# Operands of the split matmuls moved to multiples of 512 bytes, and the merge stage of a hybrid layer reordered

## The chip, the cores and the metric

The kernel runs on one core of one Trainium2 chip. The metric is device time in microseconds (us) of one launch, as the median of several runs. A separate execution was recorded by the hardware profiler; all rows below come from that one. Engines are named as in the profile: PE is the matmul engine TensorE, PEld its weight loads, DVE is VectorE, ACT is ScalarE, POOL is GpSimd, and SP (SyncE) issues most of the DMAs.

## What is computed

One layer over 1024 tokens of width 1024, in fp32: a swiglu feed-forward block (FFN1, inner width 2816), a mixer with two branches (an RWKV-7 recurrence and dilated causal attention) whose outputs are gated and merged, a second swiglu block (FFN2), and a small gated embedding term at the end. The part around the reordering is this:

```python
x = x + 0.5 * swiglu(rms_norm(x, ffn1_norm), ffn1_w_gate, ffn1_w_up, ffn1_w_down)
h = rms_norm(x, mix_norm)
z_rwkv, z_attn, z_gate = jnp.split(h @ w_in, [RWKV_COLS, RWKV_COLS + ATTN_COLS], axis=-1)
y_rwkv = rwkv7_time_mix(z_rwkv, ...)
y_attn = dilated_attention_mix(z_attn, cos, sin, q_gain, k_gain)
g_rwkv, g_attn = jnp.split(jax.nn.sigmoid(z_gate), 2, axis=-1)
merged = g_rwkv * (y_rwkv @ w_br_rwkv) + g_attn * (y_attn @ w_br_attn)
x = x + merged @ w_out
x = x + 0.5 * swiglu(rms_norm(x, ffn2_norm), ffn2_w_gate, ffn2_w_up, ffn2_w_down)
```

## The kernel before, in words

**Split matmuls.** A large fp32 matmul is done as three in the type fp32r. An operand is stored as two tiles side by side: `split` lets ACT copy the value into the high part, and DVE or POOL subtract that from the value to get the low part (lines 236 and 237). `mm3` (lines 252 to 254) then multiplies high by high, high by low and low by high into one bank of PSUM. Weights pass through `wchunk`: a DMA on SP into the staging tile `wst`, which has two buffers, then `split` into `wsp` (or `wo`, for the output projection) with POOL doing the low part. FFN weights are loaded into `wr` and split into `wsp` too, some of them after sums of two. Activations lie in tiles `h`, `a`, `f` and `ya`. In the profile `g<-h,wsp` names the PSUM tile written, then the moving operand, then the stationary one.

**Where tiles start.** Tiles are laid one after another in each partition of SBUF, pool by pool. Several pools hold small tiles whose row is not a multiple of 512 bytes long (`nss` and `nrsy` of 16 bytes, `omu`, `carry`, `n2` and others), and they move what lies behind them. In the built program all split operands start 32, 160 or 480 bytes past a multiple of 512: `wsp` and `a` at 32; `h`, `f`, `ya` at 480; `wo`, `pT` and the embedding's operands at 160. Some stationary `h` operands are read with a stride of four columns and then start at 480, 484, 488 or 492.

**Order.** A planner, `weave`, advances several streams of Python generators and lets each emit its next piece; a piece yields its cost on PE and off PE in us, written by hand, and streams "F" are dense matmul work, the others small work. The result is then a fixed list of instructions for each engine.

**The merge** has three streams. `branch_r` multiplies the RWKV output with `w_br_rwkv`: eight blocks `b` of 128 columns in two halves of 512 tokens, each with 12 matmuls, whose result DVE multiplies by the gate in line 1696, after a load of that half of the gate into a tile `gst`. `attn_combine` (lines 1650 to 1664) writes the combine weights `f` to DRAM, loads them back as a broadcast `fb`, and DVE and POOL sum three attention outputs `ob` into `ya`, which is split. `merge_a` multiplies `ya` with `w_br_attn`, again eight blocks in two halves: six matmuls, DVE's gating (line 1721), POOL's addition of the other branch (line 1724), then the split into `h`, at once. The planner is told 1.3 us on PE and 2.6 off PE a block. In the second half each second block also loads and splits a piece of `w_out` into `wo`:

```python
G.tensor_tensor(out=s, in0=th, in1=rp, op=ALU.add)
mT[b][hf] = self.half(h2, b, hf)
self.split(mT[b][hf], s)
if hf and b % 2:
    out["W"].append(self.wcol(a["w_out"], 0, b // 2, op, "wo", 4))
yield 1.3, 2.6
```

`out_proj` comes after the merge: for two halves `n` of the columns and eight tiles `i` of 128 tokens, 24 matmuls `dn<-wo,h` each into one of three `dn` banks.

## Time and profile before

| | |
|---|---|
| median of 3 runs | 2764.57 us (2763.26 to 2764.85) |
| profiled execution, its own time | 2758.78 us |
| its span, first to last instruction | 2757.0 us |
| mean granted TensorE clock, of full | 0.960 |
| PE busy | 2557.2 us, 93% of the span, 14541 matmuls |
| PE weight loads busy | 2038.9 us, 74% |
| DVE busy | 1578.3 us, 57% |
| ACT busy | 972.9 us, 35% |
| POOL busy | 1147.6 us, 42% |
| moved by DMA | 289.19 MB |

Busy means that an instruction of the engine was under way. Matmuls follow each other in a pipeline, so the profile's duration of one is longer than the time from its start to the next one's, and PE counts as busy without being at its peak. The stages in time: FFN1's up-projection from 130 to 505 us, its down-projection to 720, the mixer from 800 to 1720, the merge from 1770 to 1850, the output projection to 1942, FFN2's up-projection from 2015 to 2405, its down-projection to 2630, the embedding term to the end.

### The profile page before, as it was taken

What the parts mean: (1) busy time and instruction counts of PE and PEld (TensorE: products, weight loads), DVE (VectorE), ACT (ScalarE), POOL (GpSimd) and SP (SyncE); (2) the same over time, 40 slices, a digit from 0 to 9 for tenths busy, and PEclk for the clock granted to TensorE, in tenths of its full rate; (3) what the DMA queues carried; (4) which work ended last, traced back from release to release, by engine and by line L of the source; (5) the groups of instructions that cost most, each with busy time, mean ns of one, the idle gap of its engine ahead of it and who ended that gap; (6) DMA issues with size and microseconds to landing.
All of it is one profiled execution on the core that took longest, in us unless ns stands there. A gap on an engine that the chain in (4) does not pass through costs nothing. (4 is left out here: it accounts for less than half of the span.)

```text
span 2757.0 us, 37053 instructions
## 1 busy us (share of the span) xinstructions
PE 2557.2 (93%) x14541; PEld 2038.9 (74%) x14541; DVE 1578.3 (57%) x2511; ACT 972.9 (35%) x1700; POOL 1147.6 (42%) x643
## 2 busy tenths in 40 slices
PE   7799999999999999889989998979799999989899
PEld 5688888777777666667876998658578888767777
DVE  4865455888715555554356335461875455578852
ACT  6333333333434323332324343421533333333541
POOL 2665555454424333332232213160565555554540
PEclk9999999999999998999989999899899999999999
DMA  5332222736333222222231101662132223363532
GB/s 185 92 91 70 84 77 92 279 119 214 129 109 89 56 65 56 65 59 54 76 111 47 59 32 55 193 222 73 44 103 77 85 77 92 129 227 117 176 122 92
DMA packets 273651, 289.19 MB, mean 105 GB/s; under 512 B 46410, under 2 KB 202668, under 8 KB 273220
## 3 DMA queue, kind: packets, MB, share of 16 engines
q1 hardware_dynamic: 266084, 274.59, 31.3%
q10 hardware_dynamic: 7392, 12.23, 1.3%
q8 instruction: 114, 1.87, 0.3%
q14 instruction: 61, 0.50, 0.1%
HBM read 222.64 MB, written 64.14 MB: 104 GB/s over the span
## 5 line engine op out<-in xcount | busy, mean ns | idle before, releaser
L237 POOL TENSOR_TENSOR wsp<-wr,wsp 128x1024 fp32r<-128x1024 f32 (+1 forms) x158 | 348.0, 2210 | 400.7 <-ACT wsp L236 361.7
L237 POOL TENSOR_TENSOR wsp<-wst,wsp 128x1024 fp32r<-128x1024 f32 x71 | 173.5, 2447 | 423.9 <-ACT wsp L236 406.9
L237 POOL TENSOR_TENSOR wsp<-ws,wsp 128x1024 fp32r<-128x1024 f32 x88 | 223.3, 2538 | 214.6 <-ACT wsp L236 210.6
L252 PE MATMUL g<-h,wsp 128*128 128x512 f32 x496 | 222.7, 449 | 8.5 <-DVE h L1696 6.7
L252 PE MATMUL g<-wsp,h 128*128 128x256 f32 (+1 forms) x664 | 216.4, 326 | 12.8 <-ACT raw L1416 11.4
L254 PE MATMUL g<-wsp,h 128*128 128x256 f32 (+1 forms) x664 | 206.4, 311 | 0.0
L253 PE MATMUL g<-wsp,h 128*128 128x256 f32 (+1 forms) x664 | 206.3, 311 | 0.0
L253 PE MATMUL g<-h,wsp 128*128 128x512 f32 x496 | 203.1, 409 | 0.0
L254 PE MATMUL g<-h,wsp 128*128 128x512 f32 x496 | 203.1, 409 | 0.0
L394 DVE TENSOR_TENSOR ws<-wr 128x512 f32<-128x512 f32 x56 | 86.5, 1553 | 197.2 <-POOL x L237 195.8
L236 ACT ACTIVATE wsp<-ws 128x1024 fp32r<-128x1024 f32 (+1 forms) x110 | 106.3, 967 | 197.7 <-PE dn L254 81.6
L236 ACT ACTIVATE wsp<-wr 128x1024 fp32r<-128x1024 f32 (+1 forms) x158 | 133.5, 851 | 96.6 <-DVE wr L738 37.9
L252 PE MATMUL dn<-wsp,h 128*128 128x512 f32 x360 | 145.0, 407 | 13.1 <-DVE x L779 5.5
L252 PEld LDWEIGHTS g<-wsp,h 128*128 128x128 f32 x664 | 137.5, 207 | 25.2 <-ACT raw L1416 12.0
L253 PE MATMUL dn<-wsp,h 128*128 128x512 f32 x360 | 144.7, 402 | 4.7 <-POOL wsp L237 4.5
L254 PE MATMUL dn<-wsp,h 128*128 128x512 f32 x360 | 143.7, 401 | 0.0
L253 PEld LDWEIGHTS g<-wsp,h 128*128 128x128 f32 x664 | 137.9, 208 | 3.9 <-issue 0.2
L254 PEld LDWEIGHTS g<-wsp,h 128*128 128x128 f32 x664 | 137.2, 207 | 4.1 <-issue 0.2
L252 PEld LDWEIGHTS g<-h,wsp 128*128 128x128 f32 x496 | 96.3, 194 | 42.4 <-issue 9.0
L254 PE MATMUL tr<-h,wsp 128*128 128x512 f32 x320 | 126.4, 395 | 0.0
L254 PE MATMUL dn<-h,wsp 128*128 128x512 f32 x320 | 126.3, 395 | 0.0
L252 PE MATMUL tr<-h,wsp 128*128 128x512 f32 x320 | 126.3, 395 | 0.0
(465 smaller groups left out, 6639.2 us busy)
## 6 DMA issues: line engine op xcount, KB each, us to landing
wr<-ffn_w_down SPq DMA_DIRECT2D x44, 1024.0 KB
wst<-w_in SPq DMA_DIRECT2D x60, 512.0 KB
wr<-ffn_w_gate SPq DMA_DIRECT2D x44, 512.0 KB
wr<-ffn_w_up SPq DMA_DIRECT2D x44, 512.0 KB
actD<-act SPq DMA_DIRECT2D x44, 512.0 KB
a<-actD SPq DMA_DIRECT2D x12, 1024.0 KB
gate<-gst SPq DMA_DIRECT2D x26, 256.0 KB
wst<-ffn_w_down SPq DMA_DIRECT2D x10, 512.0 KB
```

The source lines that it names most:

```text
L236: nc.scalar.activation(dst[:, 0], src, AF.Copy)
L237: (lo_eng or nc.vector).tensor_tensor(out=dst[:, 1], in0=src, in1=dst[:, 0].bitcast(F32), op=ALU.subtract)
L252: mm(ps, lhsT=l[0], rhs=r[0], start=first, stop=False)
L253: mm(ps, lhsT=l[0], rhs=r[1], start=False, stop=False)
L254: mm(ps, lhsT=l[1], rhs=r[0], start=False, stop=last)
L394: self.nc.vector.tensor_tensor(out=out, in0=R[:, i], in1=R[:, j], op=op)
```

## The change

Small tiles leave the pools that hold split operands: they go to the constants' pool `cp` or to the pool `hp` that lives through the kernel, or are made 64 columns wide of which a few are used. After that every split operand starts at a multiple of 512 bytes (the stationary ones read with a stride of four at 0, 4, 8 or 12 past one). `pi`, the token positions, is loaded at the start in place of in the mixer.

In `branch_r` the gate comes in whole blocks of 1024 tokens, one block ahead, through the staging tile `wst`. In `merge_a` the splits of a block are emitted after the next block's addition; in the first half DVE adds and not POOL; the pieces of `w_out` are loaded in the first half; and the planner is told 0.4 us off PE. A new stream, `out_early`, computes three output-projection tiles once the first half of the merge is done, and `out_proj` takes these as they are.

```diff
+def later(cond, make):
+    yield cond
+    yield from make()
...
-        y = self.t(pool, shape, tag + "y")
-        u = self.t(pool, shape, tag + "u")
+        if tag == "grs":
+            y, u = self.t(self.cp, shape, "grsy"), self.t(self.hp, shape, "grsu")
+        elif tag == "ars":
+            y, u = (self.t(self.hp, shape, tag + n) for n in "yu")
+        elif tag == "nrs":
+            y, u = (self.t(pool, [P, 64], tag + n)[:, :shape[1]] for n in "yu")
+        else:
+            y = self.t(pool, shape, tag + "y")
+            u = self.t(pool, shape, tag + "u")
...
-            self.ss = self.t(sp, [P, 4], "nss", bufs=2)
+            self.ss = self.t(sp, [P, 64], "nss", bufs=2)[:, :4]
...
-        omu = self.t(sp, [P, 14], "omu")
+        omu = self.t(self.cp, [P, 14], "omu")
...
-        carry = {}
+        carry = self.t(self.cp, [P, 14], "carry")
...
-        nb = self.t(sp, [64, 16], "nb")
+        nb = self.t(self.hp, [64, 16], "nb")
...
-        pi = self.t(sp, [P, NT], "pi", dt=I32)
+        pi = self.t(self.hp, [P, NT], "pi", dt=I32)
...
+        def tanh(b):
+            t = self.t(self.wp, [P, T], "wst", bufs=2)
+            nc.sync.dma_start(t, gateD[b])
+            return t
+
+        th = tanh(0)
...
+            nxt = tanh(b + 1) if b < KB - 1 else None
...
-                th = self.t(mx, [P, HALF], "gst2", bufs=2)
-                nc.sync.dma_start(th, gateD[b, :, hf * HALF:(hf + 1) * HALF])
+                hsl = slice(hf * HALF, (hf + 1) * HALF)
...
-                nc.vector.scalar_tensor_tensor(out=rp[b // 2][hf][:, b % 2], in0=th, scalar=1.0, in1=ps, op0=ALU.add,
+                nc.vector.scalar_tensor_tensor(out=rp[b // 2][hf][:, b % 2], in0=th[:, hsl], scalar=1.0, in1=ps, op0=ALU.add,
                                                op1=ALU.mult)
...
+            th = nxt
...
+        last = None
+
+        def finish():
+
+            b, hf, s = last
+            mT[b][hf] = self.half(h2, b, hf)
+            self.split(mT[b][hf], s)
+            if b == KB - 1:
+                out["mT", hf] = True
...
-                G.tensor_tensor(out=s, in0=th, in1=rp, op=ALU.add)
-                mT[b][hf] = self.half(h2, b, hf)
-                self.split(mT[b][hf], s)
-                if hf and b % 2:
+                (G if hf else V).tensor_tensor(out=s, in0=th, in1=rp, op=ALU.add)
+                if last:
+                    finish()
+                last = b, hf, s
+                if hf == 0 and b % 2:
                     out["W"].append(self.wcol(a["w_out"], 0, b // 2, op, "wo", 4))
-                yield 1.3, 2.6
+                yield 1.3, 0.4
+        finish()
         out["merged"] = True
+
+    def out_early(self, mT, pp, out):
+
+        yield lambda: ("mT", 0) in out
+        W = out["W"]
+        for i in range(3):
+            ps = self.t(pp, [P, HALF], "dn", bufs=3)
+            for kb in range(KB):
+                w = W[kb // 2][:, :, kb % 2]
+                self.mm3(ps, self.hs(mT, kb, i * P, P), (w[:, 0], w[:, 1]), kb == 0, kb == KB - 1)
+                yield 0.65, 0
+            out["early"][i] = ps
...
-    def out_proj(self, mT, x, W, sp, pp, ready):
+    def out_proj(self, mT, x, W, early, sp, pp, ready):
...
-                ps = self.t(pp, [P, HALF], "dn", bufs=3)
-                for kb in range(KB):
-                    w = W[n][kb // 2][:, :, kb % 2]
-                    self.mm3(ps, self.hs(mT, kb, i * P, P), (w[:, 0], w[:, 1]), kb == 0, kb == KB - 1)
+                if n == 0 and i in early:
+                    ps = early[i]
+                else:
+                    ps = self.t(pp, [P, HALF], "dn", bufs=3)
+                    for kb in range(KB):
+                        w = W[n][kb // 2][:, :, kb % 2]
+                        self.mm3(ps, self.hs(mT, kb, i * P, P), (w[:, 0], w[:, 1]), kb == 0, kb == KB - 1)
...
-                   ["F", self.merge_a(ya, h2, D_["gate"], wr, out, op)], br], lambda: "merged" in out)
+                   ["F", self.merge_a(ya, h2, D_["gate"], wr, out, op)], br,
+                   ["F", later(lambda: out["mT"] is not None and ("mT", 0) in out, lambda: self.out_early(out["mT"], pp, out))]],
+                  lambda: "merged" in out and len(out["early"]) == 3)
...
+    k.hp = hp
```

(`cp` and `hp` get more tiles in the same way: `hw0`, `ka2`, `rki`, `n2`, `bon`, `PC`, `gst` of the group norm, `gvar`, `pf`, `ass`, `nm`. The PSUM pool of the `dn` banks is opened ahead of the merge.)

Three places show how instructions move. A name ends in the buffer's number; what stands in brackets is the counters that a row waits for. First PE near the end of the merge. In the kernel before, the last `ya` blocks (`g<-ya,wsp`) and the output projection's first tile (`dn<-wo,h`) stand like this:

```order
L252 MATMUL g_15208<-ya_2268_14796,wsp_14827 128x512
L253 MATMUL g_15208<-ya_2268_14796,wsp_14827 128x512
L254 MATMUL g_15208<-ya_2268_14796,wsp_14827 128x512
L253 MATMUL dn_15279<-wo_15162,h_2307_15045 128x512 [waits Pool_49]
L254 MATMUL dn_15279<-wo_15162,h_2307_15045 128x512
L252 MATMUL dn_15279<-wo_15162,h_2309_15057 128x512
L253 MATMUL dn_15279<-wo_15162,h_2309_15057 128x512
L254 MATMUL dn_15279<-wo_15162,h_2309_15057 128x512
L252 MATMUL dn_15279<-wo_15191,h_2311_15069 128x512 [waits Activation_49]
L252 MATMUL g_15225<-ya_2267_14795,wsp_14827 128x512 [waits DVE_49]
L253 MATMUL g_15225<-ya_2267_14795,wsp_14827 128x512
L254 MATMUL g_15225<-ya_2267_14795,wsp_14827 128x512
```

In the changed kernel, PE at the same place, with two tiles in work (`dn_15139` and `dn_15253`):

```order
L265 MATMUL dn_15139<-wo_15122,h_2311_15136 128x512 [waits Activation_49]
L266 MATMUL dn_15139<-wo_15122,h_2311_15136 128x512
L267 MATMUL dn_15139<-wo_15122,h_2311_15136 128x512
L265 MATMUL dn_15253<-wo_15062,h_2293_15057 128x512
L265 MATMUL g_15220<-ya_2252_14781,wsp_14813 128x512 [waits DVE_49]
L266 MATMUL g_15220<-ya_2252_14781,wsp_14813 128x512
L267 MATMUL g_15220<-ya_2252_14781,wsp_14813 128x512
L265 MATMUL g_15220<-ya_2253_14782,wsp_14813 128x512
L266 MATMUL g_15220<-ya_2253_14782,wsp_14813 128x512
L267 MATMUL g_15220<-ya_2253_14782,wsp_14813 128x512
L265 MATMUL g_15235<-ya_2252_14781,wsp_14813 128x512 [waits DVE_49]
```

Seven `dn` matmuls stood ahead of the last `ya` block before; now 31 do, all 24 of the first tile and seven of the second.

Second, SP's queue from the attention outputs `ob` to the first broadcasts `fb`. Before:

```order
L1630 DMA ob_14799<-o_3562 128x3x512 [waits DMAHW4_49]
L1630 DMA ob_14801<-o_3562 128x3x512 [waits DMAHW5_49,DMAHW0_49]
L1690 DMA gst_2281_14850<-gate_3560 128x512 [waits DMAHW1_49,DVE_49]
L1690 DMA gst_2283_14866<-gate_3560 128x512 [waits DMAHW2_49,DVE_49]
L1650 DMA f_3564<-ce_14806 32x3x128 [waits DVE_49]
L1715 DMA wr_15034<-gate_3560 128x4x512 [waits PE_49]
L1690 DMA gst_2285_14882<-gate_3560 128x512 [waits DMAHW1_49,DVE_49]
L1659 DMA fb_14894<-f_3564 64x3x512 [waits DMAHW6_49,DMAHW3_49]
L1659 DMA fb_14894<-f_3564 64x3x512 [waits DMAHW7_49]
```

Changed, where `wst<-gate` is a whole gate block of `branch_r`:

```order
L257 DMA wst_14806<-w_br_attn 128x2x512 [waits DVE_49]
L1661 DMA f_3564<-ce_14792 32x3x128 [waits DMAHW5_49,DVE_49]
L257 DMA wst_14811<-w_br_attn 128x2x512
L1744 DMA wr_15008<-gate_3560 128x4x512 [waits PE_49]
L1698 DMA wst_14820<-gate_3560 128x1024 [waits DMAHW4_49,Pool_49]
L1670 DMA fb_14876<-f_3564 64x3x512 [waits DMAHW5_49,DMAHW1_49]
L1670 DMA fb_14876<-f_3564 64x3x512 [waits DMAHW2_49]
L1698 DMA wst_14850<-gate_3560 128x1024 [waits DMAHW3_49,DMAHW0_49,DVE_49]
L1670 DMA fb_14912<-f_3564 64x3x512 x2
```

Both loads of `w_br_attn` and a gate block that waits for a counter of POOL now stand ahead of the first `fb`; the two `gst` loads between are gone, and the load of the second merge gates `wr` stays where it was.

Third, POOL in the first half of the merge. Before, with `ob` the attention combine and L1724 the addition:

```order
L1662 TENSOR_TENSOR ob_14970<-ob_14970,fb_14972 128x512 [waits DMAHW6_49,DMAHW0_49,DMAHW7_49,DVE_49,Pool_49]
L1724 TENSOR_TENSOR h_2200_14469<-wr_15034,h_2200_14469 128x512 [waits DMAHW4_49,DVE_49]
L1724 TENSOR_TENSOR h_2200_14469<-wr_15034,h_2200_14469 128x512 [waits DVE_49]
L1662 TENSOR_TENSOR ob_15007<-ob_15007,fb_15009 128x512 [waits DMAHW3_49,DMAHW2_49,DMAHW4_49,Activation_49,Pool_49]
L1724 TENSOR_TENSOR h_2202_14471<-wr_15034,h_2202_14471 128x512 [waits DVE_49] x2
L1724 TENSOR_TENSOR h_2204_14473<-wr_15084,h_2204_14473 128x512 [waits DMAHW6_49,DVE_49]
L237 TENSOR_TENSOR wo_15162<-wst_15160,wo_15162 128x1024 [waits DMAHW7_49,Activation_49]
L1724 TENSOR_TENSOR h_2204_14473<-wr_15084,h_2204_14473 128x512 [waits DVE_49]
L237 TENSOR_TENSOR wo_15191<-wst_15189,wo_15191 128x1024 [waits DMAHW0_49,Activation_49]
```

Changed:

```order
L1673 TENSOR_TENSOR ob_14948<-ob_14948,fb_14950 128x512 [waits DMAHW1_49,DMAHW0_49,DMAHW2_49,DVE_49,Pool_49]
L1673 TENSOR_TENSOR ob_14983<-ob_14983,fb_14985 128x512 [waits DMAHW4_49,DMAHW3_49,DMAHW5_49,DVE_49,Pool_49]
L250 TENSOR_TENSOR wo_15033<-wst_15031,wo_15033 128x1024 [waits DMAHW6_49,Activation_49]
L250 TENSOR_TENSOR wo_15062<-wst_15060,wo_15062 128x1024 [waits DMAHW7_49,Activation_49]
L250 TENSOR_TENSOR wo_15093<-wst_15091,wo_15093 128x1024 [waits DMAHW1_49,Activation_49]
L250 TENSOR_TENSOR wo_15122<-wst_15120,wo_15122 128x1024 [waits DMAHW2_49,Activation_49]
L1753 TENSOR_TENSOR h_2188_14457<-wr_15125,h_2188_14457 128x512 [waits DMAHW3_49,DVE_49]
L1753 TENSOR_TENSOR h_2188_14457<-wr_15125,h_2188_14457 128x512 [waits DVE_49]
```

The additions are no longer on POOL in the first half, and the four splits of `wo` follow one another ahead of the second half's additions (now line 1753).

## Rows read from the trace of the kernel before

**Rows 1.** Windows by stage: window, length, busy us (instructions) by engine, TensorE clock, DMA share, GB/s.

```profile
130.00:505.00 375.00, 375.00 (x1610) 301.88 (x1610) 207.61 (x219) 124.49 (x177) 220.00 (x117) 1.00 0.29 89
505.00:720.00 215.00, 200.24 (x847) 158.71 (x846) 190.84 (x253) 86.40 (x132) 104.65 (x46) 0.96 0.57 195
800.00:1270.00 470.00, 430.25 (x3752) 309.20 (x3751) 240.16 (x560) 156.00 (x311) 156.56 (x127) 0.93 0.25 66
...
1770.00:1850.00 80.00, 54.65 (x188) 39.59 (x187) 50.68 (x59) 16.42 (x23) 42.43 (x24) 0.87 0.68 197
...
2015.00:2405.00 390.00, 390.00 (x1675) 313.99 (x1674) 218.93 (x227) 130.78 (x186) 232.81 (x121) 1.00 0.29 90
```

**Rows 2.** Timeline of PE, start and length in us, in the merge.

```profile
1777.02 0.63 PE L253 MATMUL g<-h,wsp 128*128 128x512 f32 x1
...
1778.30 0.63 PE L253 MATMUL g<-h,wsp 128*128 128x512 f32 x1
```

**Rows 3.** Timeline of PE at 802.76 us, read to 803.3:804.4 and to 803.3:804.8.

```profile
802.76 1.88 PE L903 MATMUL t<-Qn,BK 128*128 128x512 f32 x4
...
802.76 2.31 PE L903 MATMUL t<-Qn,BK 128*128 128x512 f32 x5
```

**Rows 4.** Windows of four stretches without a gap on PE.

```profile
1850.96:1894.05 43.09, 43.09 (x186) 34.75 (x185) 11.85 (x12) 4.13 (x5) 12.51 (x6) 1.00 0.40 142
2685.42:2751.30 65.88, 65.88 (x289) 54.07 (x288) 17.80 (x26) 7.71 (x13) 0.00 (x0) 1.00 0.26 92
2633.34:2655.80 22.46, 22.46 (x100) 18.58 (x99) 11.06 (x14) 8.23 (x15) 10.74 (x8) 1.00 0.31 111
1538.57:1559.60 21.03, 21.03 (x180) 21.03 (x179) 8.70 (x17) 5.29 (x10) 5.32 (x2) 1.00 0.12 39
```

**Rows 5.** The chain that ended last, 1770 to 1852 us: start, length, what.

```profile
1776.77 8.39 DMA fb<-f
...
1793.78 8.16 DMA fb<-f
...
1807.64 1.69 POOL h L1724
...
1838.46 1.74 POOL h L1724
```

**Rows 6.** Waits of PE, 1770 to 1852 us: total, times, longest.

```profile
PE g L252 <- DVE h L1696: 13.6, 5, 4.1
```

**Rows 7.** Groups of PE by shape, whole span: count, busy us, mean ns.

```profile
L252 PE MATMUL g<-h,wsp 128*128 128x512 f32 x496 | 222.7, 449 | 8.5 <-DVE h L1696 6.7 <-DVE z L875 1.8
...
L252 PE MATMUL g<-wsp,h 128*128 128x256 f32 x576 | 181.6, 315 | 12.1 <-ACT raw L1416 11.4 <-ACT gst L1416 0.7
...
L252 PE MATMUL dn<-wsp,h 128*128 128x512 f32 x360 | 145.0, 407 | 13.1 <-DVE x L779 5.5 <-ACT wsp L236 4.5 <-ACT h L236 2.9
...
L252 PE MATMUL dn<-wsp 128*128 128x512 f32 x264 | 105.6, 401 | 1.9 <-ACT wsp L236 1.9
...
L254 PE MATMUL dn<-wo,h 128*128 128x512 f32 x80 | 32.1, 401 | 0.0
```

**Rows 8.** Tile `pi` (start us after the duration) and DVE's first row.

```profile
L1351 ACTq DMA_DIRECT2D pi<-positions x1: 393/393/393, 505.8 to 505.8; - x1
L1353 DVE CAST pf<-pi x1: 158/158/158, 511.3 to 511.3; 128x8 f32<-128x8 int32 x1
...
9.75 0.17 DVE L300 TENSOR_SCALAR nss<-nss 128x4 f32<-128x4 f32 x1 [9.75 <-ACT nsq L261]
```

**Rows 9.** Groups of all engines by shape, 1770 to 1852 us.

```profile
L1724 POOL TENSOR_TENSOR h<-wr,h 128x512 f32<-128x512 f32 x13 | 19.6, 1519 | 14.1 <-DVE wr L1721 14.1
...
L1721 DVE SCALAR_TENSOR_TENSOR wr<-wr,g 128x512 f32<-128x512 f32 x15 | 10.1, 679 | 3.8 <-PE g L254 3.8
...
L237 POOL TENSOR_TENSOR wsp<-wst,wsp 128x1024 fp32r<-128x1024 f32 x3 | 7.6, 2542 | 13.6 <-ACT wsp L236 13.6
...
L1664 DVE TENSOR_TENSOR ob<-ob 128x512 f32<-128x512 f32 x4 | 4.3, 1085 | 0.1
```

More of the change, by code (lines that the diff above doesn't have):

```diff
@@ L842, in rwkv @@
         nc.scalar.dma_start(wl[64:128], a["rwkv_a2"])
-        omu = self.t(sp, [P, 14], "omu")
+        omu = self.t(self.cp, [P, 14], "omu")
         nc.vector.tensor_scalar(out=omu, in0=self.pc[:, PC_MU:PC_MU + 14], scalar1=-1.0, scalar2=1.0, op0=ALU.mult,
                                 op1=ALU.add)
-        hw0 = self.t(sp, [P, 8], "hw0")
+        hw0 = self.t(self.cp, [P, 8], "hw0")
         nc.vector.tensor_scalar(out=hw0, in0=self.pc[:, PC_W0:PC_W0 + 8], scalar1=0.5, scalar2=None, op0=ALU.mult)
-        ka2 = self.t(sp, [P, 2, 4], "ka2")
+        ka2 = self.t(self.cp, [P, 2, 4], "ka2")
         nc.vector.tensor_scalar(out=ka2[:, 0], in0=self.pc[:, PC_KA:PC_KA + 4], scalar1=0.5, scalar2=None, op0=ALU.mult)
@@ L851, in rwkv @@
                                 op0=ALU.mult, op1=ALU.add)
-        rki = self.t(sp, [P, 4, 2], "rki")
+        rki = self.t(self.cp, [P, 4, 2], "rki")
         for hb in range(4):
@@ L872, in zblock @@
             else:
-                nc.scalar.activation(u[:, 0:1], carry[blk], AF.Copy)
+                nc.scalar.activation(u[:, 0:1], carry[:, blk:blk + 1], AF.Copy)
             nc.scalar.activation(u[:, 1:], ps, AF.Copy, scale=mu)
@@ L877, in zblock @@
             if hf == 0:
-                cr = self.t(sp, [P, 1], f"carry{blk}")
-                nc.scalar.activation(cr, u[:, HALF:HALF + 1], AF.Copy)
-                carry[blk] = cr
+                nc.scalar.activation(carry[:, blk:blk + 1], u[:, HALF:HALF + 1], AF.Copy)
             yield 0.65, 0
@@ L1003, in wkv_a @@
         V.scalar_tensor_tensor(out=b2, in0=ta, scalar=1.0, in1=kk, op0=ALU.add, op1=ALU.mult)
-        n2 = self.t(sp, [P, 2, 4], "n2")
+        n2 = self.t(self.cp, [P, 2, 4], "n2")
         V.tensor_scalar(out=n2, in0=pst, scalar1=1e-24, scalar2=None, op0=ALU.max)
@@ L1097, in wkv_a @@
             PE.matmul(psb[:, 2 * i:2 * i + 2], lhsT=rk[:, i * P:(i + 1) * P], rhs=rki[:, hb], start=True, stop=True)
-        bon = self.t(sp, [P, 4, 2], "bon", bufs=2)
+        bon = self.t(self.cp, [P, 4, 2], "bon", bufs=2)
         A.activation(bon.rearrange("p i h -> p (i h)"), psb[:, 0:8], AF.Copy)
-        PC = self.t(sp, [P, 8], "PC", bufs=2)
+        PC = self.t(self.cp, [P, 8], "PC", bufs=2)
         A.activation(PC, Pe[:, :, 64], AF.Copy)
@@ L1286, in wkv_c @@
         i4 = lambda t: t.rearrange("p (i f) -> p i f", i=4)
-        st = self.t(sp, [P, 4, 2], "gst")
+        st = self.t(self.cp, [P, 4, 2], "gst")
         bc = lambda t: t[:, :, :, None].to_broadcast([P, 4, 2, 64])
@@ L1300, in wkv_c @@
         yield 0, 1.0
-        var = self.t(sp, [P, 4, 2], "gvar")
+        var = self.t(self.cp, [P, 4, 2], "gvar")
         V.tensor_reduce(out=var, in_=hs_(sq), axis=AX.X, op=ALU.add)
@@ L1861, in mixer, with merged @@
         return out, br
-    def merged(self, h2, D_, out, br, wr, op):
+    def merged(self, h2, D_, out, br, wr, op, pp):
+        out["early"], out["mT"] = {}, None
         with self.pool("mg", side="right") as sp1, self.pool("cb") as sp:
@@ L1958 @@
         op = ops.enter_context(k.pool("op"))
-        mT = k.merged(hp, D_, out_, br, wr, op)
+        f2p = ExitStack()
+        pp = f2p.enter_context(k.pool("f2p", space=PSUM))
+        mT = k.merged(hp, D_, out_, br, wr, op, pp)
     wg, wu = a["ffn2_w_gate"], a["ffn2_w_up"]
@@ L1962 @@
         fb = up.enter_context(k.pool("fb2", side="right"))
-        pp = up.enter_context(k.pool("f2p", space=PSUM))
         F = {"pools": (hp, fb)}
@@ L1988, in ready @@
                 st["ops"] = k.st_pre_ops(st["R"], nq)
-        k.out_proj(mT, x, out_["W"], op, pp, ready)
+        k.out_proj(mT, x, out_["W"], out_["early"], op, pp, ready)
         ops.close()
@@ L1994 @@
     nqs.close()
+    f2p.close()
     with k.pool("fd2") as sp, k.pool("f2q", space=PSUM) as pp:
```

6 lines of the change are left out of this document (3 added, 3 removed).

## Prediction

> **What bounds the kernel now.** I read the stages first. In the table of stretches [rows 1], the two FFN up-projections (130 to 505 us and 2015 to 2405 us) show TensorE busy for all 765 us, with 1610 and 1675 instructions, 3285 in all, and a granted clock of 1.00. Nothing waits there. Each matmul takes 375.00 / 1610 = 232.9 ns, so whatever changes that figure changes the time one for one. The first down-projection (505 to 720 us) is different: DVE is busy 191 of 215 us while TensorE idles 15 us. The mixer's first half (800 to 1270 us) has TensorE busy 430 of 470 us, at a clock of 0.93. The merge (1770 to 1850 us) is the one stage where TensorE is mostly short of work: 54.65 us busy of 80, clock 0.87.
>
> Next I asked whether 232.9 ns is what the columns cost. At the half clock (1.2 GHz) four matmuls in a row start at 1777.02, 1777.44, 1777.87 and 1778.30 us [rows 2]: 427 ns, which is 512 columns at one per cycle. At 2.4 GHz 512 columns would be 213.3 ns; the FFN rows stand 19.6 ns above that. The unsplit fp32 matmuls of line 903 need two cycles a column: a row of four lasts 1.88 us and a row of five 2.31 [rows 3], so one takes 430 ns at the full clock, 3 more than its 1024 cycles. So the large excess is there only when operands are consumed at full rate. It also differs by where operands start. I took runs without a gap [rows 4]: moving operand `wsp`, stationary `wsp` (both 32 bytes past a multiple of 512), 22.46 / 99 = 226.9 ns (the length over the starts less one); moving `wsp` (32), stationary `h` (480), 65.88 / 288 = 228.8; moving `wo` (160), stationary `h` (480), 43.09 / 185 = 232.9, as much as the FFN rows, mostly with moving `h` (480) and stationary `wsp` (32); and with 256 columns, `wsp` (32) on `h` (480), 21.03 / 179 = 117.5. Offset 32 against 160, with the same stationary offset, is 4.1 ns apart: the start within 512 bytes has a price, and equal offsets have the lowest one seen.
>
> The merge I read by its chain [rows 5]: the broadcast fb of the combine weights takes 8.39 us from 1776.77, a second fb 8.16 us to 1801.9, and from 1807 the chain comes back again and again to POOL's adds of line 1724, until 1840. TensorE's longest waits there, 13.6 us in all, are for DVE's line 1696, which multiplies the loaded gates in [rows 6].
>
> **The alignment, step by step.** It adds no instruction. Every split matmul then has both operands at a multiple of 512 (the strided ones with stationary at 4, 8 or 12 bytes past, stride as before). No row shows offset 0. From above, the price is bounded by no change (232.9). From below, by the columns and the 3 ns of line 903, 216 ns, if the rest of the excess is all due to the starts. Between those ends the nearest row is the one with equal offsets near 0, the 32/32 run at 226.9, and I take it for all 512-column matmuls:
> - FFN up: 3285 x (232.9 - 226.9) = 19.7 us, whole, as nothing else is late there (POOL 220 of 375 us, DVE 208, DMA 0.29).
> - Output projection: 3 x 80 matmuls of `wo` [rows 7] x 6.0 = 1.4 us; the stage is dense.
> - Moving `wsp` on `h`: 3 x 360 = 1080 [rows 7] x 1.9 = 2.1 us. They lie in the down-projections beside a busy DVE: two thirds, 1.4 us.
> - `g<-h,wsp`, mostly the mixer: 3 x 496 = 1488 x 6.0 = 8.9 us. Many stand between short matmuls of the recurrences that wait for ACT and DVE, or ran at half clock, where rows 2 show no excess: half, 4.4 us.
> - 256 columns: 3 x 576 = 1728 [rows 7]; no equal-offset row, so half of 1.9 by columns, 0.9 ns, and half of that lands: 0.8 us.
>
> Sum 27.7 us (smaller groups left out). Its lower bound is 0. For the upper bound, 216 ns: 3285 x 16.9 = 55.5; 240 x 16.9 = 4.1; 1080 x 12.8 x 2/3 = 9.2; 3 x 264 = 792 of `dn<-wsp` [rows 7] x 10.9 x 2/3 = 5.8; 1488 x 16.9 / 2 = 12.6; 1728 x (117.5 - 109.7) / 2 = 6.7; together 94 us.
>
> A rule speaks about the size. The Trainium skill, "TensorE: Matmul & The Clock Gate", section "Back-to-back issue gap", gives the isolated gap between matmuls at the warm clock as the columns over 2.4 GHz plus 2.5 ns, 215.8 ns for 512, and names no condition on addresses. This trace differs: 226.9 to 232.9 ns. By the page the sum would be near the upper bound, if addresses are what keeps the trace from it.
>
> Small tiles (`omu`, `carry`, `n2`, `pi` and others) only move between pools. `pi`'s load goes from 505.8 us to the kernel's start, and DVE's first instruction now waits for it; DVE's first work was at 9.75 us and `pi` needed at most 5.5 us from issue to use [rows 8], so the wait for the first rows of `x` is the cover; without it, up to 5.5 us of DVE's start would show. I cost it at nothing. The same holds for `omu`, `hw0`, `ka2`: which are four operations on at most 14 columns, beside 0.17 us for DVE's first one [rows 8].
>
> **The merge.** Three things go into it.
> - Half 0 adds on DVE and not on POOL. POOL's add takes 1519 ns, DVE's add of two SBUF operands of this size 1085 ns (line 1664) [rows 9]. DVE's fastest of this size here is 679 ns (line 1721, one operand in PSUM), and at worst it is as slow as POOL's, so one add gives 0.84 us to nothing; I take 0.43, and seven of the eight adds as on the chain (rows 5 show that chain from 1807 us on): 3.0 us. DVE is busy 51 of 80 us, so it has the room.
> - Output-projection matmuls: the order above has 31 before the last `ya` block where it had 7: 24 x 0.233 = 5.6 us that TensorE does in time in which it idled. The third tile and most of the second stay behind the merge.
> - Whole gate blocks, loaded one ahead into `wst`: this can take a part of the 13.6 us of waits [rows 6]. The staging has two buffers, which the chunks of `w_br_attn` use too, so only blocks 0 to 3 are really ahead; a third, 4.5 us.
>
> Against that: on SP the load of gate block 4 now stands ahead of the first fb and waits for POOL's split of a `w_br_attn` chunk (2.5 us [rows 9]), and both chunks of `w_br_attn` (1 MB) are loaded around f, where the order before had none of them. What queues behind is fb, and behind fb the DVE and POOL combines, the `ya` splits and all `ya` matmuls. DMA moved 197 GB/s over the merge [rows 1], so 1 MB is up to 5.3 us; I take 4. The splits one block behind free DVE and ACT from waiting on each block's add; I add nothing for it. Net gain 3.0 + 5.6 + 4.5 - 4 = 9.1 us; the ends are a loss of 8 (the third rival) and a gain of 20 (all of the 13.6 us, 0.84 an add, no delay, and some overlap of these taken off).
>
> Own time 2758.78 us (span 2757.0 and 1.8 around it): 2758.8 - 27.7 - 9.1 = 2722.0. The median of the runs, 2764.57, lies 5.8 us above the profiled one, so 2728 us.
>
> **Rivals.**
> - *The starts were the whole excess.* Offset 0 cuts 2048 bytes into four pieces of 512 where every other start makes five. For: the excess vanishes at half rate [rows 2], so it lies in the supply of operands, and it falls with the start's distance past a boundary (160 to 32). Against: equal offsets still leave 13.6 ns, and no row shows it gone at full rate. Time: 2758.8 - 94 - 9 + 5.8 = 2662.
> - *The start does not matter;* the 6 ns come from what else differs between those stages. For: runs of different stages are compared. Against: 232.9 comes back at 130, 1850 and 2015 us with DMA at 0.29 to 0.40 [rows 1, 4]. Only the merge gains: 2764.6 - 9 = 2756. The Trainium skill, "SBUF — State Buffer", section "Specifications (TRN2)", gives cache lines of 16 bytes; 32, 160 and 480 are all multiples of 16, so by that rule alignment brings nothing. Rows 4 show 4 to 6 ns between such starts, which speaks against it.
> - *Slower:* fb behind gate block 4. If POOL's split of the `w_br_attn` chunk comes late, since its target buffer is freed only by branch blocks 2 and 3, fb slips by POOL's 2.5 us [rows 9] for each such chunk it waits for, plus the loads ahead of it. 4 us of slip are counted; the 9 us are gone at 13, and at 21, with the starts of no use, the time is 2764.6 + 8 = 2773. It decides from the point where the first fb, under way at 1776.77 us [rows 5], goes out 13 us later.
>
> **How the numbers follow.** Equal-offset price 0.42 (own range 2710 to 2743); whole excess 0.33; starts of no use 0.13; slower 0.12. The range 2650 to 2762 takes in the first three, down to the whole excess with the merge's gain of 20. A measurement of this kernel tells about 0.2% (5.5 us) from no change. The first two are faster by more, with most of the third: 0.83; within 0.2%: 0.07, from the edges of the last two; slower 0.10.
>
> **What would show it.** In the changed profile: FFN up at 227 ns a matmul (366 and 380 us for the two stretches) confirms the nearest row; 215 to 218 ns the first rival; 233 the second. The 256-column runs should stand at 116 to 117 ns. In the merge: no POOL adds in half 0, the first fb no later than now, 31 `dn<-wo` matmuls before the last `ya` block, and from the first fb to the dense projection some 64 us for today's 73 (1776.77 to 1850). I am wrong in mechanism if the FFN stretches shorten while their ns per matmul do not, or if the down-projections gain more than the up-projections.

## The result, and the profile after

The changed kernel takes 2737.4 us (median of 4 runs, 2731.04 to 2739.26), the kernel before 2764.71 in the same set: a ratio of 0.9896, 95% interval 0.9882 to 0.9911. It is 27.3 us faster. The forecast was 36.8 us. Two more sets of runs with the same order of TensorE's instructions, both among the experiments, gave 28.8 and 30.5 us. The profiled execution took 2731.04 us. A line of its page:

```profile
PE 2518.9 (92%) x14541; PEld 2038.0 (75%) x14541; DVE 1586.2 (58%) x2519; ACT 973.2 (36%) x1700; POOL 1148.3 (42%) x635
```

TensorE is busy 38 us less than before, for the same 14541 matmuls. Stretches of the changed kernel (columns as in [rows 1]); the first two lie in the up-projections, the third is the last `ya` blocks and the output projection, the fourth a run of 256 columns:

```profile
130.00:480.00 350.00, 350.00 (x1546) 289.79 (x1545) 205.37 (x208) 117.46 (x167) 211.95 (x113) 1.00 0.26 85
2000.00:2370.00 370.00, 370.00 (x1634) 306.49 (x1633) 218.05 (x217) 127.07 (x181) 227.31 (x119) 1.00 0.27 89
1836.57:1908.21 71.64, 71.64 (x318) 59.26 (x316) 18.38 (x34) 12.41 (x18) 10.35 (x6) 1.00 0.35 131
...
1528.35:1549.82 21.47, 21.47 (x180) 21.46 (x179) 8.93 (x17) 5.29 (x10) 5.30 (x2) 1.00 0.12 39
```

The up-projections now take 350 / 1545 = 226.5 ns a matmul, and 370 / 1633 = 226.6, against 232.9 in [rows 1]; the output projection's stretch 71.64 / 317 = 226.0, against 232.9 in [rows 4]. The run of 256 columns went the other way: 21.47 / 179 = 119.9 ns, against 117.5.

The merge is best compared from the start of the program's 10481st matmul to that of the 11001st, 520 matmuls that are the same but for two; they end in the output projection. First the kernel before, then the changed one:

```profile
1731.11:1878.95 147.84, 122.42 (x521) 90.57 (x520) 74.84 (x112) 39.22 (x71) 56.36 (x30) 0.92 0.62 194
```

```profile
1722.07:1860.83 138.76, 114.39 (x521) 87.00 (x520) 78.72 (x120) 40.24 (x79) 46.51 (x22) 0.95 0.65 209
```

It is 9.1 us shorter, and the rows show in what: TensorE is busy 8.0 us less (122.42 and 114.39) and idle only 1.0 us less (25.4 and 24.4). The granted clock is 0.95 for 0.92. Before, 43 split matmuls of the stretch last over 0.56 us in the timeline, as those of [rows 2] do at 1.2 GHz, some of them behind each of four waits of over 3 us; in the changed kernel 19 do, most of them behind one long wait. At some 0.2 us each, these 24 are the larger part of the 8.0 us.

TensorE's waits from 1755 to 1850 us, to be read beside [rows 6] (DVE's line 1714 is what was 1696, line 1750 what was 1721, which took 11.8 us before):

```profile
PE g L265 <- DVE h L1714: 10.6, 2, 9.9
PE g L265 <- DVE wr L1750: 10.4, 6, 2.4
```

The chain of the changed kernel still goes through the broadcasts, as in [rows 5]. The forecast had some 64 us from the first of them to the dense stretch of TensorE, for 73; it is 1836.57 - 1767.82 = 68.8, for 74.2 by the start of the dense run in [rows 4]:

```profile
1767.82 8.29 DMA fb<-f
```

And the additions of one size from 1760 to 1842 us, on POOL and now on DVE, to be read beside [rows 9]:

```profile
L1753 POOL TENSOR_TENSOR h<-wr,h 128x512 f32<-128x512 f32 x7 | 10.2, 1472 | 4.3 <-DVE wr L1750 4.3
...
L1753 DVE TENSOR_TENSOR h<-wr,h 128x512 f32<-128x512 f32 x7 | 7.9, 1137 | 0.0
```

The mean of 1137 ns mixes two kinds: of the eight additions on DVE in the first half six take 0.68 to 0.69 us, one 1.70 and one 2.85.

### The profile page after: what moved, and what is told of

It is laid out like the page before. It is cut to its first block, busy times and chain, and to the rows that moved or that the text cites. A ratio compares the mean times of both kernels' runs of the same rounds, so it can differ in the third digit from the quotient of the medians.

```text
span 2729.3 us, 37026 instructions
## 1 busy us (share of the span) xinstructions
PE 2518.9 (92%) x14541; PEld 2038.0 (75%) x14541; DVE 1586.2 (58%) x2519; ACT 973.2 (36%) x1700; POOL 1148.3 (42%) x635
## 4 chain that ended last, share of the span: by engine, by line
PE 48%; DVE 13%; POOL 3%; issue 2%; DMA 2%; ACT 2%; SPq 0%; ACTq 0%; DVEq 0%; POOLq 0%
PE g L265 7%; PE g L266 6%; PE g L267 6%; PE dn L266 6%; PE dn L267 6%; PE dn L265 5%; PE tr L267 1%; PE tr L265 1%; PE tr L266 1%; POOL wsp L250 1%; PE t L1055 1%; PE s L1575 1%; DMA fb<-f 1%; DVE sub L1119 1%; PE pt L1597 1%
## 5 line engine op out<-in xcount | busy, mean ns | idle before, releaser
L250 POOL TENSOR_TENSOR wsp<-wr,wsp 128x1024 fp32r<-128x1024 f32 (+1 forms) x158 | 361.5, 2296 | 374.4 <-ACT wsp L249 334.2
L265 PEld LDWEIGHTS g<-wsp,h 128*128 128x128 f32 x664 | 138.5, 209 | 28.2 <-ACT raw L1427 10.9
L463 DVE TENSOR_TENSOR act<-act,m 128x512 f32<-128x512 f32 x88 | 130.7, 1485 | 1.4
L267 PE MATMUL dn<-h,wsp 128*128 128x512 f32 x320 | 124.6, 389 | 0.0
L265 PE MATMUL dn<-h,wsp 128*128 128x512 f32 x320 | 124.5, 389 | 0.0
```

The lines of the kernel that those rows point to most:

```text
L250: (lo_eng or nc.vector).tensor_tensor(out=dst[:, 1], in0=src, in1=dst[:, 0].bitcast(F32), op=ALU.subtract)
L265: mm(ps, lhsT=l[0], rhs=r[0], start=first, stop=False)
L267: mm(ps, lhsT=l[1], rhs=r[0], start=False, stop=last)
L463: eng.tensor_tensor(out=a, in0=a, in1=v, op=ALU.mult)
```

## The experiments

**What a start costs.** A kernel of matmul rows alone, each row with one pair of starts. Each row is a line like this one (moving and stationary slices start 32 bytes, 8 elements, past a multiple of 512; three tiles alternate as in `mm3`):

```python
run([mm(ps[1][:, :512], lhsT=S[j % 3 // 2][:, 8:8+P], rhs=M[j % 3 % 2][:, 8:8+512], start=j == 0, stop=j == 47) for j in range(48)])
```

> This kernel computes nothing of the layer: it runs 38 rows of back-to-back split-type matmuls (48 of 512 columns, or 64 of 256), each row with one start of the moving and one start of the stationary operand past a multiple of 512 bytes, and writes two PSUM banks out. In the profiled kernels 512 columns took 226.7 ns at starts 0/0, 226.9 at 32/32, 228.8 at moving 32 on stationary 480, and 232.9 at 480/32 and at 160/480. Theory A, the forecast's: equal starts are what counts, so every equal pair (0, 32, 64, 128, 160, 256, 480) gives 227 and unequal pairs 229 to 233. Rival B: only the moving operand's start counts, by its distance to a boundary: 0, 32 (and 64) near 227 with any stationary start, 128, 160, 256 and 480 near 233 with any, equal ones too. Rival C: the starts are of no use and the stages differed by something else: all rows alike. For 256 columns the profiles gave 117.5 ns at 32/480 before and 120.0 at 0/0 after, so by A an unequal pair is faster there than an equal one, by B 0/32 is like 0/0, by C all are alike.

Timeline of TensorE (start, length). The period of a row is the next row's start less its own, over 48, or over 64 for 256 columns. The starts, moving/stationary, by line: L184 0/0, L185 32/32, L190 480/480, L191 0/32, L192 32/0, L195 0/128, L196 128/0, L197 0/256, L198 256/0, L201 480/32, L202 160/480, L203 32/480, L204 32/160, L205 0/16, L206 16/0; with 256 columns L210 0/0, L211 32/32, L214 32/0, L215 0/256, L218 480/32, L219 160/480.

```profile
20.48 11.05 PE L184 MATMUL q<-grid 128*128 128x512 f32 x48
31.37 11.08 PE L185 MATMUL q<-grid 128*128 128x512 f32 x48
...
85.96 11.06 PE L190 MATMUL q<-grid 128*128 128x512 f32 x48
96.87 11.35 PE L191 MATMUL q<-grid 128*128 128x512 f32 x48
108.06 11.36 PE L192 MATMUL q<-grid 128*128 128x512 f32 x48
...
141.66 11.36 PE L195 MATMUL q<-grid 128*128 128x512 f32 x48
152.85 11.31 PE L196 MATMUL q<-grid 128*128 128x512 f32 x48
163.99 11.05 PE L197 MATMUL q<-grid 128*128 128x512 f32 x48
174.88 11.05 PE L198 MATMUL q<-grid 128*128 128x512 f32 x48
...
208.16 11.37 PE L201 MATMUL q<-grid 128*128 128x512 f32 x48
219.36 11.35 PE L202 MATMUL q<-grid 128*128 128x512 f32 x48
230.56 11.16 PE L203 MATMUL q<-grid 128*128 128x512 f32 x48
241.56 11.32 PE L204 MATMUL q<-grid 128*128 128x512 f32 x48
252.71 11.35 PE L205 MATMUL q<-grid 128*128 128x512 f32 x48
263.90 11.28 PE L206 MATMUL q<-grid 128*128 128x512 f32 x48
...
308.42 7.83 PE L210 MATMUL q<-grid 128*128 128x256 f32 x64
316.09 7.83 PE L211 MATMUL q<-grid 128*128 128x256 f32 x64
...
338.98 7.63 PE L214 MATMUL q<-grid 128*128 128x256 f32 x64
346.45 7.84 PE L215 MATMUL q<-grid 128*128 128x256 f32 x64
...
369.34 7.43 PE L218 MATMUL q<-grid 128*128 128x256 f32 x64
376.60 7.70 PE L219 MATMUL q<-grid 128*128 128x256 f32 x64
```

With 512 columns, 0/0 takes 10.89 us / 48 = 226.9 ns, 480/480 227.3 and 0/256 226.9; all seven equal pairs lie from 226.9 to 227.7. Unequal pairs take more: 0/32 and 0/128 233.1, 480/32 233.3, 0/16 233.1, and 32/480 stands between, 229.2. The dearest row, not shown above, is 4/0 with 236.7. So equal starts count, and equal modulo 256 is enough. That is the forecast's theory A in a wider form; the distance to a boundary (B) does not decide, since 480/480 is as cheap as 0/0, and C falls. With 256 columns it is reversed: 0/0 7.67 / 64 = 119.8 ns, 32/0 116.7, 480/32 113.4.

**One half of the change each.** The kernel before with only the small tiles moved; and the changed kernel with only these moves taken back, for instance:

```diff
-        carry = {}
+        carry = self.t(self.cp, [P, 14], "carry")
```

> The kernel before with the small tiles moved, so that all split operands start at multiples of 512, and the merge as before. If alignment and merge add up as the two profiles suggest (FFN up-projections 20.3 us shorter, the two down-projections 5 us longer, the mixer some 4 shorter, 1.4 us lost at the start, merge 7 shorter), this one is 19 us faster than before, near 2746, and shows the loss in the down-projections (the starts of the same matmuls move from 9 us early to 5 to 6 us early between 505 and 545 us). The rival is that the loss in the down-projections belongs to the merge's changes of pools: then it is absent here and the kernel is 24 us faster, near 2741.

> The changed kernel with the small tiles where they were, so that the operands start at 32, 160 and 480 as before, and the merge as changed. By the same theory: 232.9 ns a matmul in the FFN, no loss in the down-projections, the merge 7 us shorter, 2757 us or 0.28 % faster than before. The rival, that the shorter merge comes from the cheaper matmuls in it (some 450 of them at 6 ns, 2.7 us): then only 4 us, 2760.

Alignment alone: 2738.89 us, ratio 0.9908 (0.9894 to 0.9923), 25.6 us. Merge alone: 2755.32, 0.9971 (0.9959 to 0.9982), 9.2 us. The sum of the two, 34.8, lies above the 27.3 to 30.5 of both together; the intervals, 3 to 4 us to a side each, leave it open whether anything is lost between them. They overlap, too, between the alignment alone and the whole change: what the merge's part adds to the aligned kernel, 1.5 to 6.1 us by the medians, is not clear of noise in the time. The forecast of 2746 for the alignment alone had taken a difference between two profiles for a loss; the next lines show what it was. They are the last store of activations of FFN1's up-projection and the first store of x behind the down-projection, in SP's timeline: the kernel before, the one with the merge alone, and the changed one:

```profile
507.44 3.14 SPq L524 DMA_DIRECT2D actD<-act  x2
...
749.82 2.91 SPq L1952 DMA_DIRECT2D xD<-x  x4
```

```profile
504.71 3.15 SPq L530 DMA_DIRECT2D actD<-act  x2
...
753.03 2.91 SPq L1996 DMA_DIRECT2D xD<-x  x4
```

```profile
500.88 1.65 SPq L537 DMA_DIRECT2D actD<-act  x2
...
743.76 2.79 SPq L2002 DMA_DIRECT2D xD<-x  x4
```

From the one store to the other are 242.4, 248.3 and 242.9 us. In the first two the order of TensorE's instructions is the same up to the merge, and so are the starts of the operands: this stage varies by 6 us from one execution to the next. A difference of 3 us in it between two profiles says nothing.

The merge's stretch with the merge's part alone:

```profile
1733.81:1878.05 144.24, 118.42 (x521) 89.03 (x520) 79.69 (x120) 40.59 (x79) 45.02 (x22) 0.92 0.63 201
```

That is 3.6 us shorter than in the kernel before, not the 7 expected. The two profiled executions as a whole are almost equally long, 2758.58 and 2758.78 us, so they don't show where the 9.2 us of the medians lie.

**The start of the kernel and x.** The positions' tile goes back, padded, and x comes later:

```diff
-        pi = self.t(self.hp, [P, NT], "pi", dt=I32)
+        pi = self.t(sp, [P, P], "pi", dt=I32)[:, :NT]
...
-            if (g, p) == (0, 2):
+            if (g, p) == (0, 6):
                 load_x(range(NT))
```

> The changed kernel with two edits at places far apart. The positions' tile goes back to the down-projection's pool, padded to 512 bytes, so that its load is not at the start; and x is loaded four steps later in both down-projections. Theory: the first matmul came 2.1 us later because the load of the positions holds up the parameter loads on the DMA rings; without it the first matmul is back near 10.8 us and 1.4 us are gained. And the loss at the start of the down-projections is the DMA burst (4 MB of x at 400 GB/s, 10 us, ahead of the loads of the next pieces): with x later, the same matmuls come 3 us earlier in each, 7 us in all: 2730. The rival for the second: the pieces come through DVE, ACT and POOL in a fixed time after the last activation of the up-projection, and x hides nothing: the down-projections stay, and only 1.4 us are gained, 2736.

It took 2728.01 us, ratio 0.9868 (0.9851 to 0.9884), the lowest median of all, though its interval overlaps that of the changed kernel. The changed kernel's first microseconds, all engines:

```profile
1.18 0.45 ACTq L1362 DMA_DIRECT2D pi<-positions  x1
...
5.03 0.29 SPq L212 DMA_DIRECT2D prow<-rwkv_a  x1
...
9.68 0.25 SPq L212 DMA_DIRECT2D prow<-rwkv_k_k  x1
9.68 0.17 DVE L1364 CAST pf<-pi 128x8 f32<-128x8 int32 x1 [9.68 <-DMA pi<-positions]
...
12.92 0.34 PE L214 MATMUL tr<-cst_p,prow 66*128 66x66 f32 x1 [12.92 <-DMA prow<-ple_norm]
```

The load of the positions is issued at 1.18 us, and it lands at 9.68, where DVE takes it up. SP issues a parameter load at 5.03 and the next one only at 9.68, at the same moment; it waits 4.3 us for the positions' load there. With that load late, it waits 3.2 us in all for loads of x in its place. TensorE's first matmul waits for the last of the parameter loads and starts at 12.92, in place of 10.80 in the kernel before. With the positions' load late it starts at:

```profile
11.40 0.34 PE L214 MATMUL tr<-cst_p,prow 66*128 66x66 f32 x1 [11.40 <-DMA prow<-ple_norm]
```

One execution against the other, 1.5 us are lost by the load's place. Over all thirteen profiles of the layer, the first matmul starts at 10.71 to 11.40 us in the four with the late load and at 12.56 to 12.93 in the nine with the early one. At the 251st matmul the two groups overlap, 74.95 to 77.94 and 77.14 to 79.33, and their means are still 1.5 us apart.

**x later, alone.**

> The changed kernel with x loaded four steps later in both down-projections and nothing else. The kernel with this and the late load of the positions took 2728 us. If the load of the positions at the start was all of that difference, this one is as the changed kernel within 2 us; if the x loads hold up the first pieces of the down-projections, it is 5 to 8 us faster than the changed kernel.

2729.47 us, 0.9882 (0.9866 to 0.9899), beside 2734.49 of the changed kernel on the same chip. That is the 5 us of the second guess, but the intervals overlap, and the profile does not show where: in the first down-projection the stage was no shorter than in the other executions. That x holds up the pieces is not shown. In the second down-projection, from the 13151st matmul to the 14000th, the three profiles with x late take 219.6, 220.0 and 220.4 us and the other ten 220.6 to 226.2: a hint that x late is free of a loss that some executions have, and no more than that.

**The changed kernel again.**

> The changed kernel again, unedited, beside runs of before on the same chip. Alone, the alignment gave 25.6 us and the merge 9.2 (medians). If the two are independent, as the forecast added them, this gives some 34 us, 2730; the first four runs of the changed kernel gave 27.3 us, 2737, and if that returns, part of one gain is lost when the other is there.

2734.49 us, 0.9896 (0.9880 to 0.9911), 28.8 us.

**Without the woven tiles.** The stream `out_early` is left out and `out_proj` computes all tiles:

```diff
-                   ["F", later(lambda: out["mT"] is not None and ("mT", 0) in out, lambda: self.out_early(out["mT"], pp, out))]],
-                  lambda: "merged" in out and len(out["early"]) == 3)
+                  ], lambda: "merged" in out)
```

> The changed kernel without the woven output projection tiles: all of the output projection stands behind the merge again. The forecast's theory: 24 more matmuls than before ran in time in which TensorE idled, 5.6 us, so this one is 5 to 6 us slower than the changed kernel. The rival: the merge's length is set by DVE and the fb loads, the woven matmuls push the last ya blocks back, and it is the same within 2 us.

2732.82 us, 0.9890 (0.9875 to 0.9904), no slower. But the order of TensorE shows why this says nothing on the 24 matmuls: it is the same as in the changed kernel, with 31 `dn<-wo` matmuls ahead of the last `ya` block. The stream moves nothing. Which other part brings them forward is not shown; it is neither the whole gate blocks nor the additions on DVE, since 30 and 28 stand ahead without these (in the next experiment, and in the one with the additions on POOL). The merge's stretch is 138.60 us long, as in the changed kernel.

**Halves of the gates, as before.**

```diff
-            t = self.t(self.wp, [P, T], "wst", bufs=2)
-            nc.sync.dma_start(t, gateD[b])
...
+                th = self.t(mx, [P, HALF], "gst2", bufs=2)
+                nc.sync.dma_start(th, gateD[b, :, hf * HALF:(hf + 1) * HALF])
```

> The changed kernel with the gates of the first branch loaded in halves into two small tiles of their own, as before. The forecast's theory: whole blocks one ahead take a third of the waits for the gates, so this one is 3 to 5 us slower than the changed kernel. The rival, the forecast's slower case: gate block 4 and later share the two staging tiles with the chunks of w_br_attn and wait for their splits (TensorE waited 9.9 us at one place for line 1714 in the changed kernel), so halves with tiles of their own are 3 to 6 us faster, and the first fb goes out earlier than 1767 us.

2738.46 us, 0.9907 (0.9893 to 0.9921): 4.0 us slower than the changed kernel beside it by the medians, with intervals that overlap. The merge's stretch is 7.3 us longer than in the changed kernel:

```profile
1729.92:1875.94 146.02, 123.03 (x521) 90.92 (x520) 80.74 (x120) 38.98 (x71) 45.26 (x22) 0.91 0.62 196
```

TensorE idles no more here, 23.0 us for 24.4; it is busy 8.6 us longer, at a lower clock. The first broadcast goes out 44.4 us after the stretch's start, for 45.1 in the changed kernel, so a late broadcast is not what makes the stretch longer.

**Whole gate blocks alone**, on the kernel with the alignment and the merge as before.

> The kernel with the aligned operands and the merge as before, plus one part of the merge's change: whole gate blocks of the first branch through the staging tile, one ahead. Without them it took 2738.9 us; the changed kernel took 2732.8 to 2737.4 in three sets. In the changed kernel halves cost 4.0 us. If the whole gate blocks are what the merge's change gains, this one is at 2733 to 2735; if they help only together with the additions on DVE and the later splits, it stays at 2738 to 2739.

2740.91 us, 0.9919 (0.9904 to 0.9933): not faster than the alignment alone. The stretch with the alignment alone, and with the whole blocks added:

```profile
1724.33:1869.91 145.58, 119.91 (x521) 89.76 (x520) 74.67 (x112) 39.14 (x71) 56.26 (x30) 0.93 0.61 197
```

```profile
1727.91:1875.03 147.12, 116.42 (x522) 89.02 (x521) 74.04 (x112) 40.26 (x79) 57.16 (x30) 0.93 0.60 197
```

It grew by 1.5 us. In these profiles, whole blocks are worth 7 us with the rest of the merge's change and nothing without it.

**Additions of the first half on POOL again.**

```diff
-                (G if hf else V).tensor_tensor(out=s, in0=th, in1=rp, op=ALU.add)
+                G.tensor_tensor(out=s, in0=th, in1=rp, op=ALU.add)
```

> The changed kernel with the additions of the first half back on POOL. The forecast's theory: seven additions on the chain at 0.43 us each, so this one is 3 us slower than the changed kernel. The rival: the first half of the merge waits for the fb loads and for DVE, which is busy 62 of 80 us now, and POOL's additions hide in that: the same within 1.5 us, or faster.

2739.45 us, 0.9918 (0.9904 to 0.9933): slower by the medians than the changed kernel's sets by 2 to 7 us, with intervals that overlap. The merge's stretch is 5.5 us longer than in the changed kernel, more than the 3.0 forecast:

```profile
1719.07:1863.33 144.26, 116.22 (x522) 87.62 (x520) 75.73 (x112) 40.41 (x79) 57.75 (x30) 0.94 0.62 201
```

Of the 5.5 us, 3.7 are idle time of TensorE (28.0 us for 24.4), near the forecast's 3.0, and 1.8 are busy time.

**`w_br_attn` in a tile of its own.**

```diff
-        wa = [self.wchunk(a["w_br_attn"][:, q * 512:(q + 1) * 512].rearrange("(k p) n -> p k n", p=P), 2)
-              for q in range(2)]
+        ws = self.t(wr, [P, 4, HALF], "wr", bufs=2)
...
+            s = ws[:, 2 * q:2 * q + 2]
+            nc.sync.dma_start(s, a["w_br_attn"][:, q * 512:(q + 1) * 512].rearrange("(k p) n -> p k n", p=P))
```

> The changed kernel with the two chunks of w_br_attn staged in a tile of the pool wr in place of the staging tiles, so that gate block 4 and the later ones wait for no split of them and both are loaded ahead of the first fb. TensorE waited 9.9 to 13.1 us for line 1714 in the changed kernel. If that wait is on the path, this one is 3 to 6 us faster than the changed kernel; if the fb loads set the merge's end, TensorE's wait moves to the ya blocks and the time is the same within 1.5 us.

2743.53 us, 0.9926 (0.9913 to 0.9940): 6 to 11 us slower than the changed kernel's sets. The changed kernel's SP issues the two loads of `w_br_attn`, the first gates of `merge_a` into `wr`, gate block 4 and the first broadcast like this:

```profile
1756.03 0.49 SPq L257 DMA_DIRECT2D wst<-w_br_attn  x1
...
1762.44 0.43 SPq L257 DMA_DIRECT2D wst<-w_br_attn  x1
1762.92 0.47 SPq L1744 DMA_DIRECT2D wr<-gate  x1
1766.71 0.34 SPq L1698 DMA_DIRECT2D wst<-gate  x1
1767.15 1.27 SPq L1670 DMA_DIRECT2D fb<-f  x2
```

And the kernel with a tile of its own, the first broadcast and the first load of `wr`:

```profile
1764.53 1.40 SPq L1670 DMA_DIRECT2D fb<-f  x2
...
1789.18 0.59 SPq L1750 DMA_DIRECT2D wr<-gate  x1
```

The first broadcast goes out 2.6 us earlier, 3.1 counted from the stretch's start (1722.57 and 1722.07). But `w_br_attn` now holds one of the two `wr` tiles, and the first gates of `merge_a`, now behind four pairs of broadcasts in SP's queue, are loaded at 1789.18 where they were at 1762.92. From 1755 to 1850 us TensorE waits less for gate block 4 and twice as long for DVE's gating (line 1756 is what was 1750), up to 10 us at once:

```profile
PE g L265 <- DVE wr L1756: 21.5, 6, 10.0
PE g L265 <- DVE h L1714: 6.8, 1, 6.8
```

The merge's stretch is 5.7 us longer than in the changed kernel. The wait for gate block 4 was real, and this way of shortening it made a worse one:

```profile
1722.57:1867.02 144.45, 116.09 (x521) 90.18 (x520) 80.36 (x120) 40.36 (x79) 45.24 (x22) 0.92 0.61 200
```

**The three edits together.**

> The changed kernel with three edits at places far apart: the positions' load late, x loaded four steps later in both down-projections (these two gave 2728.0 us), and w_br_attn staged in a tile of its own. If they add, 2722 to 2726 us, 1.4 to 1.5 % faster than before; if the merge is set by the fb loads, 2728.

2734.05 us, 0.9892 (0.9878 to 0.9905), 6 us slower by the medians than without the tile of its own, so they don't add. Beside the kernel with that tile alone, 2743.53 us on the same chip, it is 9.5 us faster, and those two intervals don't meet: together, the late positions and the late x do gain. Its merge stretch is 148.44 us long, 4.0 us more than that kernel's, with the same order of matmuls in it. In the five profiles with the merge as in the changed kernel it is 138.5 to 139.6. So a difference of less than some 4 us in this stretch, from one profile each, shows little; the 5.5 and 7.3 us above exceed that.

## Why the prediction was right, and where it was off

The measured 2737.4 us lies in the likeliest case's own range, 2710 to 2743, and 9 us above its point. Each half alone came near its forecast by the medians: the alignment 25.6 us for 27.7, the merge 9.2 for 9.1. The alignment did so by the mechanism that was forecast; in the merge's stretch the profiles show another.

**The alignment's price.** The forecast took the row with equal starts, 226.9 ns, as the price of all 512-column matmuls, and that is what was measured: 226.5 and 226.6 in the up-projections. The term of 19.7 us came out at 9.7 and 10.9, 20.6 us: the 501st matmul and the 2026th start at 150.12 and 505.53 us before and at 150.87 and 496.54 after, the 11401st and the 13151st at 1975.95 and 2401.14 before and at 1956.74 and 2371.04 after. From the 11001st matmul to the 11401st, which holds the rest of the output projection, 1.1 us were gained, where 1.4 were forecast for all of it.

**The first rival**, the whole excess gone, is out: no pair of starts came under 226 ns. The Trainium skill, "TensorE: Matmul & The Clock Gate", section "Back-to-back issue gap", gives 215.8 ns for 512 columns as the gap of one matmul alone; these split matmuls, one behind the other, stay over 10 ns above it at every start tried, so by the measurement it is not their price. **The second**, that the starts don't matter, is out by the grid: 0/0 and 0/16 are 6 ns apart. The Trainium skill's 16-byte lines, "SBUF — State Buffer", section "Specifications (TRN2)", would have made these two alike.

**256 columns and the mixer.** This is the term of the alignment with the wrong sign. The forecast carried the saving of equal starts over to 256 columns, at half its size, and wrote a gain of 0.8 us. The price is 119.9 in place of 117.5: 1728 x 2.4 = 4.1 us, and with the same half, 2.1 lost. The mixer was to gain 4.4 + 0.8 = 5.2 us; with the sign put right 4.4 - 2.1 = 2.3. The 2901st matmul and the 10481st start at 732.35 and 1731.11 us before and 726.30 and 1722.07 after: 3.0.

**The down-projections** were to give 1.4 us. Nothing of it can be seen: from the 2026th matmul to the 2901st the two profiles without the alignment take 226.8 and 232.8 us and the eleven with it 228.6 to 235.2. **Small tiles at nothing** was wrong by 1.2 to 2.2 us at the first matmul. The named cover was the wait for x on DVE; what was late was SP's parameter loads, behind the positions' load, which the forecast had not looked at.

**The merge** was forecast at 9.1 us, and the stretch is 9.1 us shorter; that the two figures agree is luck. The forecast's gains lay in less idle time of TensorE: additions that end sooner, matmuls moved into a time without work, shorter waits for gates. Idle time fell by 1.0 us. What fell is busy time: 122.42 us before, 119.91 with the alignment alone, 114.39 with both, the last step at the same price a matmul but with a clock of 0.95 for 0.93, which the forecast had no term for. The merge's part alone shows the same: 118.42 us busy, 25.8 idle. Why the waits of the changed order leave fewer matmuls at 1.2 GHz is not shown.

How the 9.1 us divide is not settled. Taken with the alignment, the reordering is worth 145.58 - 138.76 = 6.8 us in the stretch, and alone 147.84 - 144.24 = 3.6. Its parts don't add as the forecast had them. An addition on DVE takes 1137 ns on average, 0.38 less than POOL's 1519 in [rows 9], near the 0.43 forecast, and seven make 2.7 us; yet taking them back costs 5.5 us in the stretch, taking back the whole gate blocks 7.3, and the whole blocks alone give nothing. The 5.6 us for the early output projection were not tested, since the matmuls come forward without the stream; to have them ahead is not enough, for with 30 and 28 of them ahead the stretch is 146.02 and 144.26 us long, beside 145.58 with seven. The 4 us for a late first broadcast did not come: from the first matmul of the stretch to that broadcast's issue are 1767.15 - 1722.07 = 45.1 us, against 1776.09 - 1731.11 = 45.0 before. The **slower rival** named the right queue with the wrong victim: TensorE waited 9.9 us for gate block 4, but the broadcast was on time.

The two profiles add up stage by stage. Gained are 20.6 us in the up-projections, 3.0 in the mixer, 9.1 in the merge's stretch and 1.1 behind it, 33.8 in all. Lost are 0.8 up to the 501st matmul, 2.9 in the first down-projection and 2.4 from the 13151st matmul to the end, 6.1. That leaves 27.7 us, as the spans of 2757.0 and 2729.3 have it. Of the 9.1 us that are missing from the forecast's 36.8, 6.7 lie in these last two stretches, 5.3 lost where 1.4 were to be gained, and each of the two varies by 8 us among the profiles; 2.2 lie in the mixer. How much of each part is a gain that holds in every execution is not known better than the intervals.

## What to carry to other kernels

Look at where the moving and the stationary operand start, relative to each other: small tiles between large ones shift them, and for 512-column matmuls at full rate equal starts were worth 6 ns of 233, in a kernel with thousands of them 20 us. Take the same numbers again for each width, since 256 columns wanted the opposite. Before a stage's difference between two profiles is explained, take the stage's own spread from two executions of the same code. And where a stage gets shorter, look whether the engine idles less or is busy less, with the granted clock beside it: here a change that was meant to cut idle time left it as it was and ran with a higher clock.

## What the runs showed that was not expected

- Starts equal modulo 256 bytes are enough: 0/256 takes 226.9 ns, 0/128 233.1.
- For 256 columns starts equal modulo 256 bytes are the dearest tried (119.7 to 120.0 ns), and 480/32 is the cheapest (113.4), which with 512 columns is among the dearest (233.3).
- A load of 4 KB, the positions, took from 1.18 to 9.68 us to land at the kernel's start, and SP's parameter loads stood still behind it from 5.03 to 9.68.
- In the merge's stretch, two parts of the change cost 5.5 and 7.3 us when taken back one at a time, and all of it together is worth 6.8 with the alignment and 3.6 without: taking back either one loses most or all of it.
- The merge's stretch got 9.1 us shorter with 1.0 us less idle time: 19 matmuls in place of 43 last as long as at 1.2 GHz.
